# Matmul with RMS norm: transposes evacuated four at a time, gamma folded in early, and a different order of the first units

## The chip, the cores and the metric

The kernel runs on one core of a Trainium2 chip. The metric is the device time of one execution in microseconds (us); lower is better. Before the change the median of four runs is 275.47 us, from 274.8 to 276.51.

A core has several engines that run side by side and wait for each other through semaphores: TensorE (PE, matrix multiplication, with its weight loads shown as PEld), VectorE (DVE), ScalarE (ACT), GpSimd (POOL, which here issues the loads of a and b) and SyncE (SP, which here issues stores). Matmul results go to a small memory called PSUM; other operands lie in SBUF.

## The reference

```python
# m = k = n = 2048; a, b, gamma in float32; eps = 1e-5
def reference(a, b, gamma, eps):
    x = np.matmul(a, b)
    rms = np.sqrt(np.mean(x ** 2, axis=-1, keepdims=True) + eps)
    return (gamma * x / rms).astype(np.float32)
```

Each row of the product is divided by its root mean square and multiplied by gamma, column by column. A row's factor is known only when all 2048 columns of that row are computed.

## The kernel before

a is cut into 16 row blocks of 128 rows, b into four column chunks of 512. Both are converted to bf16 by the load. TensorE needs a transposed, so each 128x128 piece of a row block is transposed by TensorE itself (against an identity matrix) and copied from PSUM to SBUF. A first panel computes chunks 0 and 1 for all row blocks and keeps the results as bf16 with the sum of squares so far. A second panel computes chunks 2 and 3, completes the sums and writes the output.

```python
P = 128; N_CHUNK = 512; M_BLOCKS = 16; K_TILES = 16; N_CHUNKS = 4
# pools: a_rows bufs=3, at_pool bufs=16, xs_pool bufs=16, out_pool bufs=2,
#        scratch bufs=2, xtmp_pool bufs=3, at_psum bufs=4 (PSUM), x_psum bufs=4 (PSUM)

def load_a(mb, split=1):                      # one row block of a, on the GpSimd queue
    ...
def load_b_chunk(ns, parts):                  # one column chunk of b, in so many pieces
    ...
def transpose_a(a_rows, evac_scalar=10):
    at_sb = at_pool.tile([P, K_TILES, P], bf16, name="at_sb")
    for kt in range(K_TILES):
        at_psum = at_psum_pool.tile([P, P], bf16, name="at_psum")
        nc.tensor.transpose(at_psum, a_rows[:, kt, :], identity)          # L106
        if kt < evac_scalar:
            nc.scalar.copy(out=at_sb[:, kt, :], in_=at_psum)              # L108
        else:
            nc.vector.tensor_copy(out=at_sb[:, kt, :], in_=at_psum)       # L110
    return at_sb

def matmul_chunk(at_sb, b_sb):                # 16 matmuls into one PSUM tile, L116
    ...
def evac_and_ssq(x_psum, x_dst, ssq, first):
    nc.scalar.copy(out=x_dst, in_=x_psum)                                 # L126
    nc.vector.tensor_tensor_reduce(out=sq_scratch, in0=x_dst, in1=x_dst,  # L128
        scale=1.0, scalar=0.0 if first else ssq,
        op0=mult, op1=add, accum_out=ssq)

def compute_rstd(ssq):                        # sqrt on ScalarE, reciprocal on VectorE
    ...
def scale_and_store(mb, j, src, rstd, o_sb, store_engine, splits=1):
    w = N_CHUNK // splits
    for s in range(splits):
        sl = ds(j * N_CHUNK + s * w, w)
        nc.vector.scalar_tensor_tensor(out=o_sb[:, sl], in0=src[:, ds(s * w, w)],   # L156
            scalar=rstd, in1=gamma_f32[:, sl], op0=mult, op1=mult)
        store_engine.dma_start(out=out_tiled[mb][:, sl], in_=o_sb[:, sl])

a_rows_tiles[0] = load_a(0, split=2)
b_chunks[0] = load_b_chunk(0, parts=K_TILES)
a_rows_tiles[1] = load_a(1)
a_rows_tiles[2] = load_a(2)
load_gamma()                                  # on the SyncE queue
b_chunks[1] = load_b_chunk(1, parts=4)
at_tiles[0] = transpose_a(a_rows_tiles.pop(0))

for mb in range(M_BLOCKS):                    # first panel
    if mb + 3 < M_BLOCKS:
        a_rows_tiles[mb + 3] = load_a(mb + 3)
    if mb + 1 < M_BLOCKS:
        at_tiles[mb + 1] = transpose_a(a_rows_tiles.pop(mb + 1))
    if mb == 4:    b_chunks[2] = load_b_chunk(2, parts=2)
    elif mb == 10: b_chunks[3] = load_b_chunk(3, parts=2)
    ...
    for j in range(2):
        x_psum = matmul_chunk(at_tiles[mb], b_chunks[j])
        evac_and_ssq(x_psum, x_stage[mb][:, j, :], ssq_tiles[mb], first=(j == 0))

for mb in range(M_BLOCKS):                    # second panel
    # chunk 2: matmul_chunk, evac_and_ssq into x_tmp; chunk 3: matmul_chunk, left in PSUM
    nc.scalar.activation(out=sq_scratch, in_=x_psum_last, func=Square, accum_out=ssq_last)  # L217
    nc.vector.tensor_tensor(out=ssq, in0=ssq, in1=ssq_last, op=add)                         # L223
    rstd = compute_rstd(ssq_tiles[mb])
    # scale_and_store for j = 0, 1 (x_stage), 2 (x_tmp) on SyncE's queue, 3 (PSUM) on ScalarE's;
    # splits = 2 for the last block
```

The framework takes this order as a priority: it fixes each engine's instruction order itself, and may bring an instruction forward where an earlier one is not ready by its own reckoning.

Of the kernel before, what the change touches and what calls it, by code (L numbers as in the profile page):

```python
# [12 lines left out]
def kernel(  # L13
# [8 lines left out]
    nc = tc.nc  # L22
    fp32 = mybir.dt.float32
    bf16 = mybir.dt.bfloat16
# [5 lines left out]
    P = 128  # L30
    N_CHUNK = 512
    M_BLOCKS = M // P
    K_TILES = K // P
    N_CHUNKS = N // N_CHUNK
    PANELS = 2
    CHUNKS_PER_PANEL = N_CHUNKS // PANELS

    eps_val = float(eps) if not isinstance(eps, bass.AP) else 1e-5
    inv_n = 1.0 / float(N)
# [2 lines left out]
    b_pool = ctx.enter_context(tc.tile_pool(name="b_pool", bufs=N_CHUNKS))  # L42
    a_rows_pool = ctx.enter_context(tc.tile_pool(name="a_rows", bufs=3))
    at_pool = ctx.enter_context(tc.tile_pool(name="at_pool", bufs=M_BLOCKS))
    xs_pool = ctx.enter_context(tc.tile_pool(name="xs_pool", bufs=M_BLOCKS))
    out_pool = ctx.enter_context(tc.tile_pool(name="out_pool", bufs=2))
    stat_pool = ctx.enter_context(tc.tile_pool(name="stat_pool", bufs=M_BLOCKS))
    rstd_pool = ctx.enter_context(tc.tile_pool(name="rstd_pool", bufs=4))
    scratch_pool = ctx.enter_context(tc.tile_pool(name="scratch", bufs=2))
    xtmp_pool = ctx.enter_context(tc.tile_pool(name="xtmp_pool", bufs=3))  # L50

    at_psum_pool = ctx.enter_context(
        tc.tile_pool(name="at_psum", bufs=4, space=bass.MemoryType.PSUM)
    )
# [4 lines left out]
    identity = const_pool.tile([P, P], bf16)  # L59
# [5 lines left out]
    gamma_f32 = const_pool.tile([P, N], fp32)  # L65

    def load_gamma():
        nc.sync.dma_start(out=gamma_f32, in_=gamma.partition_broadcast(P))
# [2 lines left out]
    a_tiled = a.rearrange("(mo mi) k -> mo mi k", mi=P)  # L71
    out_tiled = out.rearrange("(mo mi) n -> mo mi n", mi=P)

    def load_b_chunk(ns, parts):
        b_sb = b_pool.tile([P, K_TILES, N_CHUNK], bf16, name="b_sb")
        step = K_TILES // parts
        for i in range(parts):
            ko = i * step
            if step == 1:
                nc.gpsimd.dma_start(  # L80
                    out=b_sb[:, ko, :], in_=b_tiled[ko, :, ts(ns, N_CHUNK)]
                )
            else:
                nc.gpsimd.dma_start(  # L84
                    out=b_sb[:, ds(ko, step), :],
                    in_=b_tiled[ds(ko, step), :, ts(ns, N_CHUNK)].transpose(
                        [1, 0, 2]
                    ),
                )
        return b_sb  # L90

    def load_a(mb, split=1):
        a_rows = a_rows_pool.tile([P, K_TILES, P], bf16, name="a_rows")
        kt_per = K_TILES // split
        for i in range(split):
            nc.gpsimd.dma_start(  # L96
                out=a_rows[:, ts(i, kt_per), :],
                in_=a_tiled[mb][:, ts(i, kt_per * P)],
            )
        return a_rows  # L100

    def transpose_a(a_rows, evac_scalar=10):
        at_sb = at_pool.tile([P, K_TILES, P], bf16, name="at_sb")
        for kt in range(K_TILES):
            at_psum = at_psum_pool.tile([P, P], bf16, name="at_psum")
            nc.tensor.transpose(at_psum, a_rows[:, kt, :], identity)  # L106
            if kt < evac_scalar:
                nc.scalar.copy(out=at_sb[:, kt, :], in_=at_psum)  # L108
            else:
                nc.vector.tensor_copy(out=at_sb[:, kt, :], in_=at_psum)  # L110
        return at_sb

    def matmul_chunk(at_sb, b_sb):
        x_psum = x_psum_pool.tile([P, N_CHUNK], fp32, name="x_psum")
        for kt in range(K_TILES):
            nc.tensor.matmul(  # L116
                x_psum,
                lhsT=at_sb[:, kt, :],
                rhs=b_sb[:, kt, :],
                start=(kt == 0),  # L120
                stop=(kt == K_TILES - 1),
            )
        return x_psum

    def evac_and_ssq(x_psum, x_dst, ssq, first):
        nc.scalar.copy(out=x_dst, in_=x_psum)  # L126
        sq_scratch = scratch_pool.tile([P, N_CHUNK], bf16, name="sq_scratch")
        nc.vector.tensor_tensor_reduce(  # L128
            out=sq_scratch,
            in0=x_dst,  # L130
            in1=x_dst,
            scale=1.0,
            scalar=0.0 if first else ssq,
            op0=mybir.AluOpType.mult,
            op1=mybir.AluOpType.add,
            accum_out=ssq,
        )

    def compute_rstd(ssq):
        rstd = rstd_pool.tile([P, 1], fp32, name="rstd")  # L140
        rms = rstd_pool.tile([P, 1], fp32, name="rms")
        nc.scalar.activation(  # L142
            out=rms,
            in_=ssq,
            func=mybir.ActivationFunctionType.Sqrt,
            bias=eps_tile,
            scale=inv_n,
        )
        nc.vector.reciprocal(rstd, rms)  # L149
        return rstd  # L150

    def scale_and_store(mb, j, src, rstd, o_sb, store_engine, splits=1):
        w = N_CHUNK // splits
        for s in range(splits):
            sl = ds(j * N_CHUNK + s * w, w)
            nc.vector.scalar_tensor_tensor(  # L156
                out=o_sb[:, sl],
                in0=src[:, ds(s * w, w)],
                scalar=rstd,
                in1=gamma_f32[:, sl],  # L160
                op0=mybir.AluOpType.mult,
                op1=mybir.AluOpType.mult,
            )
            store_engine.dma_start(out=out_tiled[mb][:, sl], in_=o_sb[:, sl])

    a_rows_tiles = {}
    b_chunks = {}
    a_rows_tiles[0] = load_a(0, split=2)
    b_chunks[0] = load_b_chunk(0, parts=K_TILES)
    a_rows_tiles[1] = load_a(1)  # L170
    a_rows_tiles[2] = load_a(2)
    load_gamma()
    b_chunks[1] = load_b_chunk(1, parts=4)

    at_tiles = [None] * M_BLOCKS
# [2 lines left out]

    at_tiles[0] = transpose_a(a_rows_tiles.pop(0))

    for mb in range(M_BLOCKS):
        nxt_load = mb + 3
        if nxt_load < M_BLOCKS:
            a_rows_tiles[nxt_load] = load_a(nxt_load)
        if mb + 1 < M_BLOCKS:
            at_tiles[mb + 1] = transpose_a(a_rows_tiles.pop(mb + 1))

        if mb == 4:
            b_chunks[2] = load_b_chunk(2, parts=2)
        elif mb == 10:  # L190
            b_chunks[3] = load_b_chunk(3, parts=2)

        x_stage[mb] = xs_pool.tile(
            [P, CHUNKS_PER_PANEL, N_CHUNK], bf16, name="x_stage"
        )
        ssq_tiles[mb] = stat_pool.tile([P, 1], fp32, name="ssq")
        for j in range(CHUNKS_PER_PANEL):
            x_psum = matmul_chunk(at_tiles[mb], b_chunks[j])
            evac_and_ssq(
                x_psum, x_stage[mb][:, j, :], ssq_tiles[mb], first=(j == 0)  # L200
            )

    for mb in range(M_BLOCKS):
        last_block = mb == M_BLOCKS - 1
        x_tmp = None
        x_psum_last = None
        for j in range(CHUNKS_PER_PANEL, N_CHUNKS):
            x_psum = matmul_chunk(at_tiles[mb], b_chunks[j])
            if j < N_CHUNKS - 1:
                x_tmp = xtmp_pool.tile([P, N_CHUNK], bf16, name="x_tmp")  # L210
                evac_and_ssq(x_psum, x_tmp, ssq_tiles[mb], False)
            else:
                x_psum_last = x_psum

        ssq_last = rstd_pool.tile([P, 1], fp32, name="ssq_last")
        sq_scratch = scratch_pool.tile([P, N_CHUNK], bf16, name="sq_scratch")
        nc.scalar.activation(  # L217
            out=sq_scratch,
            in_=x_psum_last,
            func=mybir.ActivationFunctionType.Square,  # L220
            accum_out=ssq_last,
        )
        nc.vector.tensor_tensor(  # L223
            out=ssq_tiles[mb],
            in0=ssq_tiles[mb],
            in1=ssq_last,
            op=mybir.AluOpType.add,
        )
        rstd = compute_rstd(ssq_tiles[mb])

        o_sb = out_pool.tile([P, N], fp32, name="o_sb")
        splits = 2 if last_block else 1
        for j in range(CHUNKS_PER_PANEL):
            scale_and_store(
                mb, j, x_stage[mb][:, j, :], rstd, o_sb,
                store_engine=nc.sync, splits=splits,
            )
        scale_and_store(
            mb, N_CHUNKS - 2, x_tmp, rstd, o_sb,
            store_engine=nc.sync, splits=splits,  # L240
        )
        scale_and_store(
            mb, N_CHUNKS - 1, x_psum_last, rstd, o_sb,
            store_engine=nc.scalar, splits=splits,
        )
        x_stage[mb] = None
        ssq_tiles[mb] = None
        at_tiles[mb] = None
# [35 lines left out]
```

## Time and profile before

| | us |
|---|---|
| median of four runs | 275.47 |
| the profiled execution, device time | 276.01 |
| its span, first to last instruction | 274.2 |
| TensorE busy | 251.5 |
| VectorE busy | 100.4 |
| ScalarE busy | 74.0 |
| 1024 matmuls of 512 columns (L116), busy | 240.3 |
| 256 transposes (L106), busy | 37.9 |
| 160 copies of a transpose on ScalarE (L108), each | 0.295 |
| 96 copies of a transpose on VectorE (L110), each | 0.220 |
| 48 casts of a result chunk on ScalarE (L126), each | 0.585 |
| 48 squares with sum on VectorE (L128), each | 0.69 to 0.75 |
| 60 multiplications by factor and gamma, 512 columns (L156), each | 0.75 |

The mean granted clock of TensorE is 0.963 of full speed. The span and the device time differ by 1.8 us. Busy times of TensorE count each matmul from its start to its end, and matmuls overlap in the pipeline, so the sum of busy times of matmuls and transposes can be longer than the time in which they run. The distance of one start to the next says what a matmul costs. The chain of waits is followed back from the last instruction, at each step to what released it.

### The profile page before, as it was taken

The numbers are of one execution on the slowest core, as the hardware profiler recorded it, in microseconds if no ns is written. First come the engines' busy times: TensorE is split into PE (matmuls) and PEld (weight loads), VectorE is DVE, ScalarE is ACT, GpSimd is POOL, SyncE is SP. The second block draws the span as 40 slices with busy tenths as digits, with TensorE's granted clock in tenths as the row PEclk, the third lists the DMA queues.
The fourth block names the chain that finished last, engine by engine and source line by source line (L and its number), as shares of the span: only waits on it lengthen the run. The fifth ranks groups of instructions, "written<-read, shape, count | busy, mean of one in ns | idle before, by whom it ended". The sixth has DMA issues, their size and how long they took to land.

```text
span 274.2 us, 3428 instructions
## 1 busy us (share of the span) xinstructions
PE 251.5 (92%) x1280; PEld 118.4 (43%) x1280; DVE 100.4 (37%) x293; ACT 74.0 (27%) x258; POOL 24.9 (9%) x47
## 2 busy tenths in 40 slices
PE   0775989999999999999999999999999999999970
PEld 0313435554445554455554444444444444444430
DVE  0102123232233232233232216555555555555554
ACT  1205014343234343234331142222222222222220
POOL 7580122000000000000000000000000000000000
PEclk9965699999999999999999999999999999999997
DMA  7999999999542334440000004444444444444444
GB/s 191 196 194 206 209 214 205 207 209 215 103 75 36 49 72 79 76 75 5 1 0 2 0 0 154 155 153 153 153 155 153 153 153 155 153 153 154 157 153 153
DMA packets 20977, 34.83 MB, mean 127 GB/s; under 512 B 1760, under 2 KB 10976, under 8 KB 20832
## 3 DMA queue, kind: packets, MB, share of 16 engines
q0 software_dynamic: 11024, 16.78, 35.6%
q1 hardware_dynamic: 7488, 13.63, 14.8%
q10 hardware_dynamic: 2448, 4.20, 4.6%
q8 instruction: 10, 0.16, 0.2%
q14 instruction: 7, 0.06, 0.1%
HBM read 34.60 MB, written 16.78 MB: 187 GB/s over the span
## 4 chain that ended last, share of the span: by engine, by line
PE 84%; DMA 9%; POOL 3%; DVE 1%; issue 1%; ACT 0%; DVEq 0%; POOLq 0%; ACTq 0%
PE x_psum L116 78%; PE at_psum L106 6%; DMA b_sb<-in_b_dram 6%; DMA a_rows<-in_a_dram 3%; POOL b_sb L80 2%; DVE o_sb L156 1%; POOL b_sb L84 1%; POOL a_rows L96 1%; ACT sq_scratch L217 0%; DVEq L279 0%; ACT rms L142 0%; POOL identity masks.py:199 0%; POOL identity masks.py:197 0%; DVE rstd L149 0%; DVE ssq L223 0%
## 5 line engine op out<-in xcount | busy, mean ns | idle before, releaser
L116 PE MATMUL x_psum<-b_sb,at_sb 128*128 128x512 bf16 x1024 | 240.3, 383 | 3.9 <-DMA b_sb<-in_b_dram 3.4
L116 PEld LDWEIGHTS <-at_sb 128*128 128x128 bf16 x1024 | 99.4, 98 | 118.1 <-issue 11.0
L106 PE MATMUL at_psum<-identity,a_rows 128*128 128x128 bf16 x256 | 37.9, 229 | 10.5 <-DMA a_rows<-in_a_dram 10.5
L126 ACT CAST x_stage<-x_psum 128x512 bf16<-128x512 f32 x32 | 18.7, 585 | 95.7 <-PE x_psum L116 95.7
L106 PEld LDWEIGHTS <-a_rows 128*128 128x128 bf16 x256 | 23.6, 101 | 28.8 <-DMA a_rows<-in_a_dram 11.8
L108 ACT COPY at_sb<-at_psum 128x128 bf16<-128x128 bf16 x160 | 29.0, 295 | 11.9 <-PE at_psum L106 11.9
L128 DVE CUSTOM_DVE_ANT_0 sq_scratch<-x_stage,ssq 128x512 bf16<-128x512 bf16 x16 | 12.0, 752 | 45.2 <-ACT x_stage L126 45.2
L110 DVE COPY at_sb<-at_psum 128x128 bf16<-128x128 bf16 x96 | 16.7, 220 | 29.8 <-PE at_psum L106 29.4
L128 DVE CUSTOM_DVE_ANT_0 sq_scratch<-x_stage 128x512 bf16<-128x512 bf16 x16 | 11.1, 692 | 40.9 <-ACT x_stage L126 40.9
L156 DVE SCALAR_TENSOR_TENSOR o_sb<-x_stage,rstd,gamma_f 128x512 f32<-128x512 bf16 (+1 forms) x34 | 22.9, 717 | 0.7
L217 ACT ACTIVATE sq_scratch<-x_psum 128x512 bf16<-128x512 f32 x16 | 9.6, 597 | 46.8 <-DMA out_dram<-o_sb 38.1
L126 ACT CAST x_tmp<-x_psum 128x512 bf16<-128x512 f32 x16 | 9.4, 586 | 34.6 <-PE x_psum L116 34.6
L223 DVE TENSOR_TENSOR ssq<-ssq,ssq_last 128x1 f32<-128x1 f32 x16 | 2.6, 160 | 43.4 <-ACT sq_scratch L217 43.4
L96 POOL DMA_DIRECT2D a_rows<-in_a_dram x17 | 9.2, 543 | 89.8 <-PE at_psum L106 89.2
L128 DVE CUSTOM_DVE_ANT_0 sq_scratch<-x_tmp,ssq 128x512 bf16<-128x512 bf16 x16 | 11.9, 742 | 2.7 <-ACT x_tmp L126 2.7
L156 DVE SCALAR_TENSOR_TENSOR o_sb<-x_tmp,rstd,gamma_f 128x512 f32<-128x512 bf16 (+1 forms) x17 | 12.1, 714 | 0.0
L156 DVE SCALAR_TENSOR_TENSOR o_sb<-x_psum,rstd,gamma_f 128x512 f32<-128x512 f32 (+1 forms) x17 | 12.0, 713 | 0.0
L80 POOL DMA_DIRECT2D b_sb<-in_b_dram x16 | 8.5, 542 | 4.1 <-DMA a_rows<-in_a_dram 3.1
L84 POOL DMA_DIRECT2D b_sb<-in_b_dram x8 | 6.5, 830 | 0.1
L142 ACT ACTIVATE rms<-ssq,eps_tile 128x1 f32<-128x1 f32 x16 | 4.7, 294 | 3.4 <-DVE ssq L223 3.4
L149 DVE RECIPROCAL rstd<-rms 128x1 f32<-128x1 f32 x16 | 2.6, 164 | 6.9 <-ACT rms L142 6.9
L128 DVE DVE_READ_ACCUMULATOR2_ANT ssq<- 128x1 f32 x48 | 4.0, 82 | 0.0
(10 smaller groups left out, 6.6 us busy)
## 6 DMA issues: line engine op xcount, KB each, us to landing
out_dram<-o_sb SPq DMA_DIRECT2D x45, 256.0 KB, 2.7
a_rows<-in_a_dram POOLq DMA_DIRECT2D x15, 512.0 KB, 7.3
b_sb<-in_b_dram POOLq DMA_DIRECT2D x4, 1024.0 KB, 20.2
out_dram<-o_sb ACTq DMA_DIRECT2D x15, 256.0 KB, 2.8
b_sb<-in_b_dram POOLq DMA_DIRECT2D x16, 128.0 KB, 5.1
b_sb<-in_b_dram POOLq DMA_DIRECT2D x4, 512.0 KB, 13.7
gamma_f<-in_gamma_dram SPq DMA_DIRECT2D x1, 1024.0 KB, 4.7
out_dram<-o_sb SPq DMA_DIRECT2D x6, 128.0 KB, 2.0
```

The source lines that it names most:

```text
L80: nc.gpsimd.dma_start(out=b_sb[:, ko, :], in_=b_tiled[ko, :, ts(ns, N_CHUNK)])
L84: nc.gpsimd.dma_start(out=b_sb[:, ds(ko, step), :], in_=b_tiled[ds(ko, step), :, ts(ns, N_CHUNK)].transpose([1, 0, 2]),)
L96: nc.gpsimd.dma_start(out=a_rows[:, ts(i, kt_per), :], in_=a_tiled[mb][:, ts(i, kt_per * P)],)
L106: nc.tensor.transpose(at_psum, a_rows[:, kt, :], identity)
L108: nc.scalar.copy(out=at_sb[:, kt, :], in_=at_psum)
L110: nc.vector.tensor_copy(out=at_sb[:, kt, :], in_=at_psum)
L116: nc.tensor.matmul(x_psum, lhsT=at_sb[:, kt, :], rhs=b_sb[:, kt, :], start=(kt == 0), stop=(kt == K_TILES - 1),)
L126: nc.scalar.copy(out=x_dst, in_=x_psum)
L128: nc.vector.tensor_tensor_reduce(out=sq_scratch, in0=x_dst, in1=x_dst, scale=1.0, scalar=0.0 if first else ssq, op0=mybir.AluOpType.mult, ...
L142: nc.scalar.activation(out=rms, in_=ssq, func=mybir.ActivationFunctionType.Sqrt, bias=eps_tile, scale=inv_n,)
L156: nc.vector.scalar_tensor_tensor(out=o_sb[:, sl], in0=src[:, ds(s * w, w)], scalar=rstd, in1=gamma_f32[:, sl], op0=mybir.AluOpType.mult, o ...
L217: nc.scalar.activation(out=sq_scratch, in_=x_psum_last, func=mybir.ActivationFunctionType.Square, accum_out=ssq_last,)
```

## The change

It has four parts.

- Transposes: four go side by side into one PSUM tile, and one copy of 512 columns evacuates them; groups alternate between ScalarE and VectorE. This is to have fewer copies and fewer waits for PSUM buffers.
- The result chunks: ScalarE takes the squares with their sum straight from PSUM, and VectorE multiplies by gamma from PSUM in the same step that makes the bf16 copy. Each chunk's sum of squares has a column of its own, and the four are added at the end. Every chunk but the very last is evacuated, chunk 3 too.
- The output: since gamma is already in, what is left is a multiplication by the row's factor, on ScalarE for chunks 0 and 2 and on VectorE for 1 and 3; stores are issued half by SyncE and half by ScalarE.
- The order: row block 3 is loaded ahead of b's second chunk, and the first four row blocks are multiplied by chunk 0 first and by chunk 1 afterwards, so that TensorE has work while chunk 1 is still arriving.

```diff
-    scratch bufs=2, xtmp_pool bufs=3
+    scratch bufs=4, xtmp_pool bufs=4
@@ transpose_a
-        for kt in range(K_TILES):
-            at_psum = at_psum_pool.tile([P, P], bf16, name="at_psum")
-            nc.tensor.transpose(at_psum, a_rows[:, kt, :], identity)
-            if kt < evac_scalar:
-                nc.scalar.copy(out=at_sb[:, kt, :], in_=at_psum)
+        for g in range(0, K_TILES, 4):
+            at_psum = at_psum_pool.tile([P, 4, P], bf16, name="at_psum")
+            for i in range(4):
+                nc.tensor.transpose(at_psum[:, i, :], a_rows[:, g + i, :], identity)
+            if g % 8 == 0:
+                nc.scalar.copy(out=at_sb[:, ds(g, 4), :], in_=at_psum)
             else:
-                nc.vector.tensor_copy(out=at_sb[:, kt, :], in_=at_psum)
+                nc.vector.tensor_copy(out=at_sb[:, ds(g, 4), :], in_=at_psum)
@@ evac_and_ssq becomes evac_chunk(x_psum, x_dst, ssq4, j)
-        nc.scalar.copy(out=x_dst, in_=x_psum)
-        nc.vector.tensor_tensor_reduce(out=sq_scratch, in0=x_dst, in1=x_dst, ..., accum_out=ssq)
+        nc.scalar.activation(out=sq_scratch, in_=x_psum, func=Square, accum_out=ssq4[:, j : j + 1])
+        nc.vector.tensor_tensor(out=x_dst, in0=x_psum, in1=gamma_f32[:, ts(j, N_CHUNK)], op=mult)
@@ compute_rstd
+        nc.vector.reduce_sum(ssq, ssq4, axis=X)
@@ scale_and_store becomes rstd_scale_and_store
-            nc.vector.scalar_tensor_tensor(o_sb, src, rstd, gamma_f32, mult, mult)
+            # last block, chunk 3 (still in PSUM, without gamma): scalar_tensor_tensor as before
+            elif on_scalar:      # j even
+                nc.scalar.activation(out=o_sb[:, sl], in_=srcs, func=Copy, scale=rstd)
+            else:                # j odd
+                nc.vector.tensor_scalar_mul(out=o_sb[:, sl], in0=srcs, scalar1=rstd)
             store_engine.dma_start(out=out_tiled[mb][:, sl], in_=o_sb[:, sl])
+            # store_engine: nc.sync for j even, nc.scalar for j odd
@@ loads
     a_rows_tiles[2] = load_a(2)
+    a_rows_tiles[3] = load_a(3)
     load_gamma()
     b_chunks[1] = load_b_chunk(1, parts=4)
@@ first panel
+    EARLY = 4
+    units = [(mb, 0) for mb in range(EARLY)] + [(mb, 1) for mb in range(EARLY)]
+    for mb in range(EARLY, M_BLOCKS):
+        units += [(mb, 0), (mb, 1)]
+    transposed = 1
+    for i, (mb, j) in enumerate(units):
+        if i + 1 < len(units) and units[i + 1][0] == transposed:
+            if transposed + 3 < M_BLOCKS:
+                a_rows_tiles[transposed + 3] = load_a(transposed + 3)
+            at_tiles[transposed] = transpose_a(a_rows_tiles.pop(transposed))
+            transposed += 1
+        if (mb, j) == (4, 0):    b_chunks[2] = load_b_chunk(2, parts=2)
+        elif (mb, j) == (10, 0): b_chunks[3] = load_b_chunk(3, parts=2)
+        x_psum = matmul_chunk(at_tiles[mb], b_chunks[j])
+        evac_chunk(x_psum, x_stage[mb][:, j, :], ssq_tiles[mb], j)
@@ second panel: evac_chunk for chunks 2 and 3 of every block, but for the last chunk of the last block
```

## The prediction

> **What bounds the kernel now.** I read the page's busy shares first, then the chain that ended last, then the same two by stage.
>
> Busy shares (engine, busy us, share, instructions) and the start of the chain's shares by line:
>
> ```profile
> PE 251.5 (92%) x1280; PEld 118.4 (43%) x1280; DVE 100.4 (37%) x293; ACT 74.0 (27%) x258; POOL 24.9 (9%) x47
> ...
> PE 84%; DMA 9%; POOL 3%; DVE 1%; issue 1%; ACT 0%; DVEq 0%; POOLq 0%; ACTq 0%
> ```
>
> TensorE is the bound; VectorE (37%) and ScalarE (27%) are far from it. So moving work between those two is worth nothing in itself: only what TensorE waits for, what TensorE itself does, and the tail after its last matmul can change the time. The chain in order of time (start, length, what) shows where TensorE becomes the chain and stays it:
>
> ```profile
> 16.83 2.21 POOL b_sb L84 x3
> 19.04 16.42 DMA b_sb<-in_b_dram
> 35.50 6.42 PE x_psum L116 x29
> ...
> 50.12 0.22 PE at_psum L106 x4
> 50.34 0.65 PE x_psum L116 x3
> 50.99 0.36 PE at_psum L106 x2
> 51.34 0.22 PE x_psum L116
> 51.56 0.12 PE at_psum L106 x2
> 51.68 0.22 PE x_psum L116
> 51.90 0.12 PE at_psum L106 x2
> 52.02 0.22 PE x_psum L116
> 52.24 0.29 PE at_psum L106 x3
> ```
>
> Until 35.50 us the kernel waits for data, the last piece of b's second chunk; from there to 265.99 us TensorE has no gap. Three stages follow.
>
> *Start, 0 to 35.5 us.* Matmuls of L116 alone by stretch (start:end, length, PE busy and count, PEld busy and count, granted clock, DMA share, GB/s):
>
> ```profile
> 0.00:35.45 35.45, 14.95 (x35) 3.99 (x36) 0.76 1.10 199
> 35.45:41.50 6.05, 6.00 (x28) 2.72 (x28) 1.00 1.06 214
> 41.50:49.70 8.20, 7.81 (x33) 3.04 (x32) 1.00 1.22 205
> ```
>
> Only 35 of 1024 matmuls and 48 of 256 transposes (three blocks) are done in the first 35.45 us. DMA runs at 199 to 214 GB/s all the while. At 205 GB/s a chunk of b (2.1 MB as bf16) takes 10.2 us, a row block of a (0.52 MB) 2.6 us. The second row block lands at 22.9 us, and what TensorE does next is held by b's second chunk. The clock is at half besides:
>
> ```profile
> 22.91 3.87 PE L106 MATMUL at_psum<-identity,a_rows 128*128 128x128 bf16 x23 [2.28 <-DMA a_rows<-in_a_dram]
> ...
> 27.84 1.86 PE L116 MATMUL x_psum<-b_sb,at_sb 128*128 128x512 bf16 x4 [1.06 <-DMA b_sb<-in_b_dram]
> ...
> 31.00:32.00 1.00, 1.00 (x4) 0.33 (x3) 0.00 (x0) 0.00 (x0) 0.00 (x0) 0.50 1.24 206
> 32.00:33.00 1.00, 1.00 (x8) 0.57 (x7) 0.30 (x3) 0.00 (x0) 0.00 (x0) 0.86 1.24 206
> ```
>
> (The last two are one-microsecond stretches of all engines; the 0.50 and 0.86 near the end are the clock.) Full speed returns about 4.3 us after the matmuls of 27.84 start.
>
> *First panel.* Each block of 32 matmuls and 16 transposes takes 8.20 us. The second panel has 568 matmuls in 122.61 us, so 0.2159 us each; 32 take 6.91. The 16 transposes therefore take 1.29, or 81 ns each. But the chain above has four in 0.22, 55 ns each, and then 0.36 for two, 0.29 for three: after the first four (the pool has four PSUM buffers, one transpose each) every further one waits for a copy out of PSUM. 16 at 55.6 ns would be 0.89 us, so the wait costs about 0.40 us a block.
>
> *Tail.* The last matmul ends at 265.99, the end is 274.2: 8.2 us of square, root, eight half-chunk multiplications on VectorE and the last stores.
>
> [...]
>
> **The change part by part.**
>
> *Evacuation in fours.* 160 copies of 295 ns on ScalarE and 96 of 220 ns on VectorE become 32 and 32 of 512 columns. ScalarE's 512-column cast takes 585 ns, so a block costs it 2 x 0.585 = 1.17 us where it was 10 x 0.295 = 2.95. More to the point, four buffers now hold all 16 transposes of a block, so none waits for a copy of its own block: 1.29 becomes 0.89 us, 0.40 less for each block that runs in the steady state.
>
> *Order of units and one row block earlier.* The third row block is followed by the fourth, ahead of b's second chunk, and blocks 0 to 3 first use chunk 0 alone. So TensorE has work from 22.9 us that needs no second chunk. Work: block 1's transposes at half clock 16 x 0.11 (twice 55 ns) = 1.7, to 24.6. Unit (1,0) starts there; full clock some 4.3 to 5 us later, about 29.3. By then 11 matmuls at 0.43, twice 0.216; 5 more at 0.216: 30.4. Block 2's transposes 0.9 and unit (2,0) 3.45: 34.8. Block 3's the same: 39.1. If the instruction order puts block 2's transposes ahead of (1,0), TensorE waits for that row block (22.9 + 2.6 = 25.5) and everything comes about 1.3 us later, 40.4. I take the middle, **39.8 us for 64 matmuls and 64 transposes**. The second chunk lands one row block later than before, 35.5 + 2.6 = 38.1, and so in time.
>
> What is left at 39.8: before, 35 + 4.3/0.2159 = 55 matmuls are done, 969 are left (209.2 us), with 208 transposes at 81 ns (16.8): 226.0 us. After: 960 x 0.2159 = 207.3, and 192 x 0.0556 = 10.7: 218.0. The difference is **8.0 us**, of which 1.9 are matmuls, 1.3 a block of transposes done earlier and 4.8 the shorter transposes of twelve blocks.
>
> *Squares on ScalarE, gamma on VectorE.* [...] Worth 0 us off the end.
>
> *Tail.* Square to reciprocal stays (1.4 us). Then VectorE's 267.43 to 270.68 splits: four half-chunks each on two engines. But ScalarE must also issue four stores at 0.36 to 0.44 (two before). [...] Saved: 0.3 to 1.0, **0.6 us**.
>
> Sum: 275.47 - 8.0 - 0.6 = **266.9 us**.
>
> **The rivals.**
>
> *The spacing of transposes is 81 ns whatever the buffers.* [...] Against it: 0.22 for four, then visibly longer for two. It would give back 4.8: 271.7 us, inside 2%. I give it one chance in five.
>
> *The start gains nothing or much more.* Nothing, if the clock stays at half longer or the fixed instruction order makes TensorE wait for row blocks 2 and 3: before, seven of the 23 transposes at 22.91 already belong to block 2, so this order is possible. That costs the 3.2 us of matmuls and early transposes: 270.1. Much more, if the clock rises during the transposes: 48 matmuls and 48 transposes at full speed from 22.9 take 10.4 + 2.7, to 36.0, 3.8 us better: 263.1, less a wait for the last of the second chunk.
>
> *A new wait: later row blocks come too late.* The fourth block takes 2.6 us from the second chunk, and TensorE runs 8 us ahead by the end of the panel, while b's third chunk is issued between row blocks. Blocks up to 6 with three and a half chunks and gamma are 12.1 MB, so some 60 us; block 6 is wanted about 64 us. Tight but free; a miss costs 1 to 3 us. *ScalarE or VectorE as the bound* I give one in thirty; 3.9 of 6.91 us leaves room.
>
> **Range and chances.** The three main uncertainties are plus 4.8 (transposes), plus 3.2 to minus 3.8 (start) and about 1 (tail). Two bad ones together reach 275; one bad one 270 to 272; a good start 263. So 262.5 to 271.5 us. The 2% line is 270.0: faster by more 0.78, within 2% 0.20, slower 0.02.
>
> **What would show it.** In the chain: 16 transposes of a block in about 0.9 us with no pieces of 0.36; blocks of the first panel 7.8 us apart; TensorE without a gap from about 24 us instead of 35.5; last matmul about 258 us; a tail of 7 to 8 us. Wrong if blocks still stand 8.2 us apart, if TensorE waits for row blocks or b after 40 us, or if matmuls of the second panel come further apart than 0.216 us.

## The result and the profile after

The kernel after takes 265.18 us (median of 10 runs, 264.25 to 266.85), beside 274.94 us for the kernel before in the same sessions. The ratio is 0.9638, 95% interval 0.9617 to 0.966: 3.6% faster. The span of the profiled execution falls from 274.2 to 263.4 us. (Line numbers have moved: matmuls are L118, transposes L108.)

The busy shares after, from the page:

```profile
PE 243.0 (92%) x1280; PEld 116.5 (44%) x1280; DVE 73.2 (28%) x162; ACT 89.5 (34%) x212; POOL 24.8 (9%) x47
...
PE 88%; DMA 5%; POOL 2%; issue 1%; DVE 1%; ACT 1%; ACTq 0%; DVEq 0%; POOLq 0%
```

VectorE lost 27 us of work and ScalarE gained 15.5. The experiments below show that this is not where the time came from. The share of the chain held by DMA fell from 9 to 5%. The chain in order of time (start, length, what):

```profile
15.05 7.01 DMA a_rows<-in_a_dram
...
22.11 1.89 PE at_psum L108 x16
23.99 1.28 PE x_psum L118 x3
25.27 1.33 PE at_psum L108 x16
26.60 2.81 PE x_psum L118 x13
29.41 0.89 PE at_psum L108 x16
30.30 17.27 PE x_psum L118 x80
47.57 0.89 PE at_psum L108 x16
48.46 6.91 PE x_psum L118 x32
55.37 0.89 PE at_psum L108 x16
...
134.26 120.88 PE x_psum L118 x560
...
255.22 0.70 ACT sq_scratch L234 x2
```

Two things are to be seen. TensorE is the chain from 22.11 us on, 13.4 us sooner than before. And a block's 16 transposes are one piece of 0.89 us where they were seven pieces with matmuls between, 1.29 us in sum; blocks follow each other by 7.80 us (47.57 to 55.37) instead of 8.20. The first piece of transposes took 1.89 us at a granted clock of 0.50; those from 29.41 on take 0.89 at 1.00. One-microsecond stretches around the change of the clock (granted clock third from the end):

```profile
25.00:26.00 1.00, 1.00 (x10) 0.93 (x9) 0.00 (x0) 0.26 (x1) 0.00 (x0) 0.50 1.02 201
26.00:27.00 1.00, 1.00 (x13) 0.73 (x11) 0.79 (x2) 0.91 (x2) 0.10 (x1) 0.97 1.16 194
```

Full speed comes at about 26.06 us (0.97 for that microsecond), 6.2 us sooner than before (32.28, from the 0.86 of the microsecond from 32 us on). At the 39.8 us at which the prediction compared, the matmuls are:

```profile
0.00:39.80 39.80, 22.28 (x77) 0.87 1.10 204
```

77 matmuls, the last of them still running, and 64 transposes: the prediction had 64 and 64. The 64th matmul is done at 37.2 us (32 by 30.30, then 32 at 0.2159). The last matmul ends at 255.2 us, before at 265.99. The tail is 8.2 us, as before.

### The profile page after: what moved, and what is told of

It is laid out like the page before. It is cut to its first block, busy times and chain, and to the rows that moved or that the text cites. A ratio compares the mean times of both kernels' runs of the same rounds, so it can differ in the third digit from the quotient of the medians.

```text
span 263.4 us, 3263 instructions
## 1 busy us (share of the span) xinstructions
PE 243.0 (92%) x1280; PEld 116.5 (44%) x1280; DVE 73.2 (28%) x162; ACT 89.5 (34%) x212; POOL 24.8 (9%) x47
## 4 chain that ended last, share of the span: by engine, by line
PE 88%; DMA 5%; POOL 2%; issue 1%; DVE 1%; ACT 1%; ACTq 0%; DVEq 0%; POOLq 0%
PE x_psum L118 83%; PE at_psum L108 6%; DMA a_rows<-in_a_dram 5%; POOL b_sb L81 2%; ACT sq_scratch L234 0%; POOL a_rows L97 0%; DVE o_sb L180 0%; ACTq L183 0%; DVEq L294 0%; DVE o_sb L164 0%; ACT o_sb L173 0%; ACT rms L147 0%; POOL identity masks.py:199 0%; POOL identity masks.py:197 0%; DVE rstd L154 0%
## 5 line engine op out<-in xcount | busy, mean ns | idle before, releaser
L118 PE MATMUL x_psum<-b_sb,at_sb 128*128 128x512 bf16 x1024 | 228.8, 382 | 2.3 <-DMA b_sb<-in_b_dram 1.8
L118 PEld LDWEIGHTS <-at_sb 128*128 128x128 bf16 x1024 | 99.8, 98 | 123.1 <-issue 7.8
L129 ACT ACTIVATE sq_scratch<-x_psum 128x512 bf16<-128x512 f32 x63 | 37.4, 594 | 136.7 <-PE x_psum L118 136.1
L135 DVE TENSOR_TENSOR x_stage<-x_psum,gamma_f 128x512 bf16<-128x512 f32 x32 | 22.0, 688 | 67.9 <-ACT sq_scratch L129 67.9
L135 DVE TENSOR_TENSOR x_tmp<-x_psum,gamma_f 128x512 bf16<-128x512 f32 x31 | 21.4, 692 | 62.7 <-ACT sq_scratch L129 62.7
L108 PE MATMUL at_psum<-identity,a_rows 128*128 128x128 bf16 x256 | 19.2, 234 | 9.8 <-DMA a_rows<-in_a_dram 9.8
L112 DVE COPY at_sb<-at_psum 128x512 bf16<-128x512 bf16 x32 | 13.5, 420 | 44.1 <-PE at_psum L108 44.0
L108 PEld LDWEIGHTS <-a_rows 128*128 128x128 bf16 x256 | 17.4, 106 | 15.0 <-DMA a_rows<-in_a_dram 11.6
L110 ACT COPY at_sb<-at_psum 128x512 bf16<-128x512 bf16 x32 | 17.3, 587 | 10.7 <-PE at_psum L108 10.6
L173 ACT ACTIVATE o_sb<-x_stage,rstd 128x512 f32<-128x512 bf16 (+1 forms) x17 | 11.7, 696 | 3.7 <-DVE rstd L154 3.7
L173 ACT ACTIVATE o_sb<-x_tmp,rstd 128x512 f32<-128x512 bf16 (+1 forms) x17 | 11.7, 696 | 3.3 <-DVE o_sb L180 2.9
L129 ACT ACTIVATION_READ_ACCUMULATOR sq_scratch<-x_psum 128x1 f32 x63 | 12.2, 194 | 0.0
L234 ACT ACTIVATE sq_scratch<-x_psum 128x512 bf16<-128x512 f32 x1 | 0.6, 597 | 2.5 <-PE x_psum L118 2.5
```

Of the source, the lines that this page charges most:

```text
L108: nc.tensor.transpose(at_psum[:, i, :], a_rows[:, g + i, :], identity)
L110: nc.scalar.copy(out=at_sb[:, ds(g, 4), :], in_=at_psum)
L112: nc.vector.tensor_copy(out=at_sb[:, ds(g, 4), :], in_=at_psum)
L118: nc.tensor.matmul(x_psum, lhsT=at_sb[:, kt, :], rhs=b_sb[:, kt, :], start=(kt == 0), stop=(kt == K_TILES - 1),)
L129: nc.scalar.activation(out=sq_scratch, in_=x_psum, func=mybir.ActivationFunctionType.Square, accum_out=ssq4[:, j : j + 1],)
L135: nc.vector.tensor_tensor(out=x_dst, in0=x_psum, in1=gamma_f32[:, ts(j, N_CHUNK)], op=mybir.AluOpType.mult,)
```

## The experiments

The kernels below the first were each timed beside the kernel before, whose medians in these sessions were 274.97 to 275.31 us.

| kernel | us, median | ratio to before (95%) |
|---|---|---|
| after | 265.18 | 0.9617 to 0.966 |
| fours only | 269.1 | 0.9736 to 0.9802 |
| order only | 271.13 | 0.9805 to 0.9892 |
| fours and order | 265.37 | 0.9596 to 0.9678 |
| epilogue only | 275.34 | 0.9984 to 1.0039 |
| after, small copies | 265.03 | 0.9581 to 0.9658 |
| after, gamma late | 266.01 | 0.9572 to 0.9725 |
| after, extra transposes | 267.05 | 0.9608 to 0.9731 |
| after, extra matmuls | 268.3 | 0.9627 to 0.9784 |
| after, extra transposes, other order | 264.26 | 0.9565 to 0.9626 |
| after, half of the last stores | 265.24 | 0.9617 to 0.968 |
| piecewise start, 12 | 261.78 | 0.9491 to 0.9539 |
| piecewise start, 8 | 262.1 | 0.9481 to 0.9544 |

### One part at a time

**Fours only.** The kernel before with the new transposes alone:

```diff
# before, and of the change only:
+            at_psum = at_psum_pool.tile([P, 4, P], bf16, name="at_psum")
+            (four transposes into it, then one copy of 512 columns)
```

> The kernel before with only the transposes changed (four to a PSUM tile, one copy for each four). Theory (the stall of later transposes on their copies is what this part removes, 0.40 us a block): 13 blocks from 41.5 us on give 5.2 us, and some 0.6 us at the start, so about 269.7 us, blocks 7.8 us apart. Rival (transposes cost 81 ns whatever the buffers, and the whole gain is the new order): 275 us, blocks 8.2 us apart.

Measured 269.1 us, 5.9 us less. The first panel's chain:

```profile
102.77 0.89 PE at_psum L107 x16
103.66 6.91 PE x_psum L117 x32
110.57 0.89 PE at_psum L107 x16
```

16 transposes run back to back at 0.89 us, and blocks are 7.80 us apart. So 55.6 ns, a sixteenth of 0.89 us, is what a transpose costs here even 16 in a row; the 81 ns of the rival was work and wait mixed.

**Order only.** The kernel before with the new loads and the new order of the first panel:

```diff
# before, and of the change only:
+    a_rows_tiles[3] = load_a(3)        # ahead of b's second chunk
+    units = [(mb, 0) for mb in range(4)] + [(mb, 1) for mb in range(4)] + ...
```

> The kernel before with only the loads and the order of the first panel changed; transposes one to a PSUM tile, result chunks as before. Theory (the order gives matmuls to do while the second chunk arrives, and the clock rises early because TensorE is busy from 22 us on, whatever with): about 271 us, blocks 8.2 us apart, last block of the first panel some 4 to 5 us earlier than before. Rival (the clock rises early only because transposes run densely, without waits for copies): 273 us, clock at half until about 29 us.

Measured 271.13 us, 3.9 us less. The blocks keep their waits (a piece of 0.36 us for two transposes at 108.34, as before). In this run row block 1 was there at 23.5 us, and full speed came at about 27.95 (granted clock third from the end, with TensorE's busy time alone ahead of it):

```profile
27.00:28.00 1.00, 1.00 (x7) 0.54 1.08 188
28.00:29.00 1.00, 1.00 (x11) 1.00 1.23 205
```

That is 4.4 us after the first transpose and 3.7 after the first matmul behind it, although transposes here wait for copies. So the clock also rises before 29 us without dense transposes, and the rival fell.

**Fours and order together**, with squares, gamma and output as before:

```diff
# after, and of the change taken back:
-        evac_chunk(...)                # Square on ScalarE, gamma on VectorE
+        evac_and_ssq(...)              # as before, and scale_and_store as before
```

> The kernel after, but with the squares, gamma and the output as before (two of the four parts). Theory (moving work between ScalarE and VectorE is worth nothing, neither being on the path): 265.2 us, within 0.6 us of the kernel after. Rival (evacuating chunks sooner or the split output contributes): 267 us or more.

Measured 265.37 us: the kernel after within 0.2 us. The two parts add up, 5.9 + 3.9 = 9.8 against 9.6 together, within the 1.2 us by which the interval of the order alone is open to each side.

**Epilogue only.** The kernel before with only squares, gamma and output changed:

```diff
# before, and of the change only:
+        nc.scalar.activation(sq_scratch, x_psum, Square, accum_out=ssq4[:, j : j + 1])
+        nc.vector.tensor_tensor(x_dst, x_psum, gamma_f32[:, ts(j, N_CHUNK)], mult)
+        (and the output split over two engines)
```

> The kernel before with only the squares, gamma and output changed (ScalarE squares from PSUM, VectorE multiplies by gamma, output split over two engines); loads, order and transposes as before. Theory (not on the path): within 0.7 us of the kernel before, 275 us. Rival (it is part of the gain): 273 us or less.

Measured 275.34 us beside 275.31. It moves squares, scalings and stores between two engines and is worth nothing that can be seen (the interval is about 0.8 us to each side).

### Places in PSUM or fewer copies

The fours bring two things at once: PSUM places for all 16 transposes of a block, and a quarter of the copies. This kernel keeps the places and goes back to 16 copies:

```diff
-            if g % 8 == 0:
-                nc.scalar.copy(out=at_sb[:, ds(g, 4), :], in_=at_psum)
-            else:
-                nc.vector.tensor_copy(out=at_sb[:, ds(g, 4), :], in_=at_psum)
+            for i in range(4):      # ScalarE for the first 10 of 16, VectorE for the rest
+                copy(out=at_sb[:, g + i, :], in_=at_psum[:, i, :])
```

> The kernel after, four transposes to a PSUM tile, but 16 copies of 128 columns for each block instead of four of 512. Theory (what counts is that all 16 transposes of a block have a place in PSUM, not how few copies there are): 265.2 us, within 0.6 us of the kernel after, 16 transposes in 0.89 us. Rival (fewer, larger copies are what removes the wait): up to 271 us, blocks 8.2 us apart.

Measured 265.03 us, and the chain has the same pieces:

```profile
102.88 0.89 PE at_psum L108 x16
103.78 6.91 PE x_psum L119 x32
```

So the places are what counts. How many copies empty them, and how long these take beside the 6.91 us of matmuls, does not.

### The start: bytes, clock, or order

**Gamma late.** Gamma's 1.05 MB is loaded at the very start by SyncE, beside the first loads of a and b. Here it goes behind them:

```diff
-        nc.sync.dma_start(out=gamma_f32, in_=gamma.partition_broadcast(P))
+        (four pieces of 512 columns on the GpSimd queue: the first behind
+         row block 3, the others behind b's second chunk)
```

> The kernel after, with gamma's load moved from the start to the same queue as a and b: its first 512 columns behind row block 3, the rest behind b's second chunk. Theory (until 22 us TensorE waits for bytes, and gamma's 1.05 MB stands ahead of them, 5.1 us at 205 GB/s): row block 1 lands about 17 us instead of 22.1, last matmul 3.5 to 5 us earlier, about 260.7 us. Rival (the transfers are held by how fast they are issued, not by bytes): 265 us.

Measured 266.01 us: nothing gained, and the theory fell. Two stretches of the start (start:end, length, busy times of five engines, clock, DMA share, GB/s), first of the kernel after, then of this one:

```profile
1.00:5.00 4.00, 0.00 (x0) 0.00 (x0) 0.00 (x0) 1.02 (x1) 3.65 (x8) 1.00 0.82 276
...
10.00:20.00 10.00, 7.72 (x16) 1.41 (x14) 0.35 (x1) 0.08 (x1) 8.51 (x15) 0.79 1.22 204
```

```profile
1.00:5.00 4.00, 0.00 (x0) 0.00 (x0) 0.00 (x0) 1.02 (x1) 3.65 (x8) 1.00 0.52 71
...
10.00:20.00 10.00, 8.62 (x16) 1.35 (x14) 0.09 (x1) 0.00 (x0) 8.24 (x16) 1.00 1.20 193
```

276 GB/s for 4 us is 1.1 MB, in the main gamma itself. Without gamma only 71 GB/s flow in these 4 us: the GpSimd queue had hardly begun, and it went no faster afterwards. Row block 0's first half was there 2 us sooner (first transposes at 5.55 us instead of 7.59), but its second half only 0.25 us (8.60 instead of 8.85), and row block 1's transposes start at 21.98 us instead of 22.11. So gamma delayed nothing that counted. What holds the GpSimd queue to this pace was not separated: from 9.83 us on its loads of b's first chunk are issued 0.65 us apart, which is about as long as the transfer of one takes (128 KB on the page, 0.64 us at 204 GB/s), and the DMA engines are busy throughout (share 1.20 and 1.22).

**Extra work to hold the clock.** A unit (i,j) is the 16 matmuls of row block i with column chunk j. Between 16 and 22 us TensorE has one matmul of unit (0,0) for each 0.64 us of transfer, and the clock falls to half (granted 0.50 from 16 us on): the record of one such matmul grows from 0.38 us at 15.44 to 0.58 at 19.54. These two kernels fill the gaps with work that nobody uses:

```diff
# unit (0,0), after the matmul of each piece kt of b's first chunk:
+            for r in range(4 if kt < K_TILES - 1 else 30):
+                nc.tensor.transpose(d[:, r % 4, :], b_sb[:, kt, ts(r % 4, P)], identity)
# second kernel: nc.tensor.matmul(d, lhsT=identity, rhs=b_sb[:, kt, ts(r % 4, P)], ...)
```

> The kernel after with extra work without use on TensorE while b's first chunk arrives: four transposes of the piece of b just landed after each matmul of unit (0,0), and 30 at its end, into a PSUM tile that nobody reads. Theory A (transposes count as activity for the clock): the clock stays at full speed from 16 us on; gain of 0.3 to 1 us, since row block 2 lands only about 24.7 us: 264.6 us. Theory B (transposes do not count): the clock falls to half at 16 us as without them, the 30 take 3.3 us and delay row block 1, 266 to 267 us.

> As the run with extra transposes, but with ordinary matmuls of 128 columns (identity as weights) in their place. Under both theories the clock stays at full speed, and the time is 264.6 us. If the clock falls here too, neither theory holds and something other than the share of busy time sets it.

Measured 267.05 and 268.3 us: neither shows a gain. Both medians lie above the kernel after's, but the intervals overlap with its, and one run of each (265.82 and 265.49 us) is about as fast. TensorE in the first of them (start, length, engine, line, what, count, and the idle time before with its releaser):

```profile
19.84 1.56 PE L127 MATMUL at_psum<-identity,b_sb 128*128 128x128 bf16 x25
21.88 1.07 PE L108 MATMUL at_psum<-identity,a_rows 128*128 128x128 bf16 x16 [0.48 <-DMA a_rows<-in_a_dram]
25.40 1.89 PE L108 MATMUL at_psum<-identity,a_rows 128*128 128x128 bf16 x16 [2.45 <-DMA a_rows<-in_a_dram]
```

The clock did hold: granted 1.00 until 24 us, and row block 1's transposes take 1.07 us instead of 1.89, behind 30 transposes in a row (the first line shows 25 of them). But the framework's instruction order changed with the extra work. Row block 2's transposes now stand ahead of unit (1,0), TensorE waits 2.45 us for that row block, and the clock falls while it does (granted 0.95 from 24 to 25 us, 0.50 for the next two; the transposes behind the wait take 1.89 us). The kernel with extra matmuls shows the same, with 1.07 us, then a wait of 1.43 us, then 1.89 us; there the last two pieces of b's first chunk also came late (TensorE waits 0.82 and 0.62 us for them), and row block 1's transposes start only at 23.67 us. So the clock part of theory A stood, and both time forecasts failed: the first on the order, which the next kernel changes back, the second on the order and the late loads, which were not told apart.

The first of them again, with unit (1,0) put ahead of row block 2's transposes:

```diff
-        if i == 0:
-            x_psum = matmul_chunk(at_tiles[mb], b_chunks[j], first=True)
+        if i < 2:      # also unit (1,0): its matmuls, then the next transposes
+            x_psum = matmul_chunk(at_tiles[mb], b_chunks[j], first=(i == 0))
```

> The run with extra transposes once more, with unit (1,0) put ahead of the transposes of row block 2, so that TensorE need not wait for that row block. Theory (the extra transposes keep the clock up, and the loss in the first run was the wait of 2.4 us for row block 2): transposes of row block 1 in 0.9 us, unit (1,0) at full speed, 1.5 us less than the kernel after, 263.7 us. Rival (the extra work itself delays the loads or the first unit): 265.2 us or more.

Measured 264.26 us, 0.9 us less than the kernel after; the intervals of the two ratios overlap by 0.001 (0.9565 to 0.9626 and 0.9617 to 0.966), so the gain is likely and no more. Its TensorE:

```profile
22.77 1.07 PE L108 MATMUL at_psum<-identity,a_rows 128*128 128x128 bf16 x16 [0.51 <-DMA a_rows<-in_a_dram]
24.07 3.40 PE L118 MATMUL x_psum<-b_sb,at_sb 128*128 128x512 bf16 x15 [0.23 <-ACT at_sb L110]
```

The four matmuls of unit (0,0) from 18.02 to 20.21 us, all but the last with four transposes behind it, take 0.38 us each. Unit (1,0) runs at full speed: its 15 matmuls and the next transposes start 3.24 us apart (24.07 and 27.31), 0.216 us a matmul. The row block landed 0.7 us later in this run than in the one shown of the kernel after, which takes part of the gain back.

**Piecewise start.** If TensorE starves because one unit is 0.22 us of work for 0.64 us of transfer, four units at a time should cure it. The kernel also loads b's second chunk in eight pieces instead of four, and asks for row blocks 4 to 7 together, behind the matmuls of chunk 0:

```diff
-    load order: row block 0, b chunk 0, row blocks 1 to 3, b chunk 1
+    load order: row blocks 0 to 3, b chunk 0, b chunk 1
-    units (0,0), (1,0), (2,0), (3,0), (0,1), ...: one after the other
+    for j in range(2):       # four PSUM tiles open at once
+        for kt in range(12): for mb in range(4): matmul(mb, j, kt)
+        for mb in range(4):  for kt in range(12, 16): matmul(mb, j, kt)
-    b chunk 1 parts=4; a_rows bufs=3, scratch bufs=4
+    b chunk 1 parts=8; a_rows bufs=4, scratch bufs=2
```

> The kernel after with another start: row blocks 0 to 3 are loaded ahead of b's first chunk, and each piece of chunk 0 (later chunk 1) is used for all four blocks as it lands, four matmuls (0.86 us) for each 0.64 us of transfer. Theory (the start is limited by how much work the bytes landed so far allow; one unit a piece is 0.22 us of work for 0.64 us of transfer): matmuls from about 18 us without a gap, 64 matmuls and 64 transposes done at 32 to 34 us instead of 37.2, some of it given back to the four results that must be evacuated at once; 261 us. Rival (loading three row blocks ahead of b costs as much as it brings): 265 us or more.

Measured 261.78 us, ratio to before 0.9515 (0.9491 to 0.9539): the fastest version, 3.4 us below the kernel after. Its chain:

```profile
16.23 1.89 PE at_psum L108 x16
18.12 0.43 PE x_psum L218
18.55 0.22 issue
18.77 11.20 PE x_psum L218 x50
```

51 matmuls and 64 transposes are done at 30 us; the kernel after has 32 and 64 at 30.3. The last matmul ends at 251.2 us instead of 255.2. The loads' new order and smaller pieces were not tested apart from the four units at a time.

The chain of this kernel also passes through an evacuation at 31.80 us, which I read as a wait of 0.8 us. The next kernel was to remove it:

```diff
-    TOGETHER = 12
+    TOGETHER = 8
```

> The piecewise start once more, with the four row blocks together for the first 8 of 16 pieces of a chunk only (12 before); the other 8 are done block by block. Theory (a result is evacuated in about 1.4 us, square and then multiplication, and four results that end 0.86 us apart make TensorE wait for it some 0.8 us at each chunk; ending 1.73 us apart they do not): 0.5 to 1.5 us less than with 12, about 260.8 us. Rival (block by block so early, TensorE waits for pieces that have not landed): 262 us or more.

Measured 262.1 us, no difference from 261.78. The reading was wrong. In the kernel with 12, the 77 matmuls of the first four blocks that are left at 29.97 us are done at 46.4, at 0.214 us each, in a piece without idle time (84 matmuls, 18.94 us from 27.65 on), so there is no gap. The chain followed one result through its evacuation while TensorE worked on another. There was no wait to remove.

### The tail

The output's scaling is now split over two engines. The last result ends at 258.84 us, 3.6 us after the last matmul, where it was 4.7 (270.68 less 265.99), and the last issue of a store ends 4.1 us after it (259.30), where it was 5.2 (271.20). The last issues and results, before and then after:

```profile
269.81 0.87 DVE L156 SCALAR_TENSOR_TENSOR o_sb<-x_psum,rstd,gamma_f 128x256 f32<-128x256 f32 x2
270.32 0.88 ACTq L164 DMA_DIRECT2D out_dram<-o_sb  x2
```

```profile
257.19 2.11 SPq L183 DMA_DIRECT2D out_dram<-o_sb  x4
258.35 0.49 ACT L173 ACTIVATE o_sb<-x_tmp,rstd 128x256 f32<-128x256 bf16 x1
```

Yet the tail is 8.2 us in both. Does the transfer of the last 1 MB set it?

```diff
+            rows = P // 2 if mb == M_BLOCKS - 1 else P
-            store_engine.dma_start(out=out_tiled[mb][:, sl], in_=o_sb[:, sl])
+            store_engine.dma_start(out=out_tiled[mb][0:rows, sl], in_=o_sb[0:rows, sl])
```

> The kernel after, but the last row block stores only its rows 0 to 63 (as many stores, each of half the bytes; the output's last 64 rows are left out). Theory (the tail's scaling now ends 1 us sooner, but the 1.05 MB of the last block then take 3.1 us at 340 GB/s, and that sets the end): the time from the last matmul to the end falls from 8.2 to about 6.8 us, 263.8 us. Rival (scaling and issuing the stores set the end): within 0.3 us of 8.2.

Measured 265.24 us, with a tail of 263.0 less 254.97, so 8.0 us. The stretch of the tail in which the stores move, first of the kernel after, then of this one:

```profile
258.00:261.00 3.00, 0.00 (x0) 0.00 (x0) 0.07 (x1) 0.84 (x2) 0.00 (x0) 0.53 1.01 338
```

```profile
258.00:261.00 3.00, 0.00 (x0) 0.00 (x0) 0.00 (x0) 0.91 (x2) 0.00 (x0) 0.51 0.76 174
```

Half the rate, and the DMA engines still move bytes until about 261 us. The forecast of 6.8 us fell. But this does not clear the bytes, because the issues took longer in this kernel:

```profile
256.94 2.73 SPq L184 DMA_DIRECT2D out_dram<-o_sb  x4
```

SyncE's four issues take 2.73 us instead of 2.11, so the last issue ends 4.7 us after the last matmul instead of 4.1. From there to the end it is 3.3 us instead of 4.1. A store can land sooner with half the bytes: the shortest time from issue to landing is 2.1 us, where it is 2.4 in the kernel after and was 1.9 before (medians of the last stores there: 2.8, and 2.0 to 2.2). Slower issuing took that back. The kernel with gamma late has all the bytes, and its tail is 7.9 us. So the 1.1 us of faster scaling were lost between the last issue and the end; whether bytes or issues set that in the kernel after stays open.

## Why the prediction was right, point by point

**What bounds the kernel** was right. The part that only moves work between VectorE and ScalarE is worth nothing that can be seen (275.34 beside 275.31 us alone, 265.37 beside 265.18 on top of the others).

**Evacuation in fours** was right in mechanism and size: 0.89 us a block, 7.80 us between blocks, twelve blocks of 0.40 us in the kernel after. The 55.6 ns a transpose that the sum uses is a sixteenth of this 0.89 us; the trace before shows four in 0.22 us, 55 ns. The reason given, room for all 16 transposes, was the right one: with 16 small copies the chain is the same. The rival of 81 ns fell.

**The order** was right in mechanism and too small. The 64 matmuls and 64 transposes put at 39.8 us are done at 37.2. By the trace these 2.6 us are three terms. Row block 1 was there at 22.11 us and not at 22.9: 0.8 us. The mis-sized term is "full clock some 4.3 to 5 us later, about 29.3", counted from the first matmul of unit (1,0): full speed came 2.3 us after it (23.79 to 26.06), so that 2.3 us of work were done at half speed instead of 4.7: 1.2 us. And TensorE did not wait for row block 2, because three matmuls of unit (1,0) filled the time until it landed; 39.8 was the middle between 39.1 without and 40.4 with such a wait: 0.7 us.

The first two terms are in part luck. Row block 1's transposes start between 21.71 us (half of the last stores) and 23.55 us (order only) in the traces that have the same loads up to it and no extra work. And in five traces with this order and these transposes (after, fours and order, small copies, gamma late, half of the last stores) full speed comes 2.3, 1.5, 1.0, 4.1 and 2.5 us after the first matmul of unit (1,0), by the durations; counted from row block 1's first transpose it is 2.7 to 5.8 us. The 4.3 us came from one trace and lie beyond the latest of the five (by the clock record 4.4 there, 27.84 to 32.28). What sets the moment was not found.

The rival of a good start (263.1 us) had an early full speed in it, but already for row block 1's transposes, and these still ran at half. Its opposite, that TensorE waits for row block 2, did not happen here, but did in the two kernels with extra work, at 2.45 and 1.43 us.

**The tail** was wrong. "Saved: 0.3 to 1.0, 0.6 us" is 0.0. Scaling ends 1.1 us sooner, and the last issue ends 4.1 us after the last matmul instead of 5.2. But I took the time from there to the end as fixed, and it grew from 3.0 us (271.2 to 274.2) to 4.1 (259.3 to 263.4), as the last stores took 2.8 us to land instead of 2.0 to 2.2.

**The load on ScalarE and VectorE** was overestimated a little and did not matter: 50.4 and 41.1 us busy in the 120.9 us of the second panel, so 2.9 and 2.3 us a block of 6.91. With two issues of stores at their median of 0.40 us ScalarE has 3.7 us a block, where the forecast had 3.9. VectorE's scaling from bf16 takes 0.48 us, where its multiplications by factor and gamma took 0.75 before. No run shows the extra time for a factor by row that the 3.9 us, and the 0.6 us of the tail, count for each scaling on ScalarE; the runs showed 0.72 us for a scaling of 512 columns and 0.50 for one of 256, beside 0.585 for a cast of 512 before.

**No new wait for row blocks** was right: after 22.11 us the chain shows none to the last matmul.

The sum: 8.0 + 2.6 - 0.0 = 10.6 us, of the 10.8 by which the two spans differ (274.2 and 263.4). The medians differ by 9.8, because the profiled execution of the kernel before was itself about 1 us above the median of that kernel. By the medians of the separate kernels, the fours alone gave 5.9 us where their part of the sum had 4.8, and the order alone 3.9 where it had 3.2, so not all of the excess belongs to the order. That 266.9 us lies only 1.7 above the measured median is luck in part: the 0.6 us of the tail that did not come stand against the 2.6 that the start brought beyond the forecast.

## What to carry to other kernels

Before counting copies or moving them between engines, ask how many results the bound engine can put down before it must wait: 16 transposes in four PSUM tiles gave 5.9 us whatever the copies. Where data arrives slowly at the start, put as much work as there is on each piece that has landed: one unit a piece gave way to four, and that kernel gained about as much again as the new order had (3.4 us beside 3.9). Time saved ahead of a store is only saved if the store lands sooner: scaling that ended 1.1 us sooner left the tail at 8.2 us.

## What was not expected of the hardware

Extra transposes without use kept TensorE's clock at full speed, as ordinary matmuls did. In the kernel with extra transposes and the other order, the four matmuls of unit (0,0) from 18.02 to 20.21 us take 0.38 us each, as do the four from 17.87 to 21.16 us with ordinary matmuls behind them; in the kernel after, which has neither, one takes 0.58 at 19.54 us. Row block 1's 16 transposes then take 1.07 us in all three kernels with extra work, instead of 1.89. Whether transposes also *raise* the clock the runs do not settle: in the piecewise start three blocks of transposes, behind gaps of 1.48, 0.55 and 0.53 us, stayed at 1.89 us each, and full speed came within some 1.5 us of the first matmul, judging by 50 matmuls in 11.20 us.

The granted clock in the records cannot be taken alone. In the kernel with gamma late the record says 1.00, yet row block 1's 16 transposes take 1.89 us and three matmuls 1.28, exactly as in the kernel after, where it says 0.50:

```profile
21.98 1.89 PE L112 MATMUL at_psum<-identity,a_rows 128*128 128x128 bf16 x16 [1.92 <-DMA a_rows<-in_a_dram]
...
22.00:23.00 1.00, 1.00 (x10) 1.00 1.14 229
```

The kernels with the fours only and with fours and order show the same, 1.89 us at a recorded 1.00. The durations are what to read.
